# LayerNorm's running sums moved from VectorE to GpSimd, two channel tiles at a time, with the norm's chain and one pair's residuals placed differently at the seam

## The chip, the cores and the metric

The kernel runs on one core of a Trainium2 chip. The metric is the device time of one execution in microseconds; three timed runs of the kernel before gave 839.31, 839.94 and 841.18, so its time is the median, 839.94 us. Engines are named as in the profile: PE is TensorE (matmuls; PEld its weight loads), DVE VectorE, ACT ScalarE, POOL GpSimd, SP the queue that issues the loads.

## What is computed

Two residual layers on 256 tokens of width 2048, in float32. The first mixes eight retention heads and eight latent-attention heads; the second is a convolution module. The change lies where the first ends and in the second, whose reference is:

```python
def layer_conformer_conv(x, norm_g, w_in, conv_w, conv_b, ln_g, ln_b, w_out):
    h = rms_norm(x, norm_g)
    a, b, gate = jnp.split(h @ w_in, 3, axis=-1)
    u = a * jax.nn.sigmoid(b)
    u = lax.conv_general_dilated(u, conv_w[:, None, :], ..., feature_group_count=CONV_WIDTH) + conv_b
    u = jax.nn.silu(layer_norm(u, ln_g, ln_b))
    return x + (u * jax.nn.silu(gate)) @ w_out
```

The convolution is causal, has 31 taps and works on each of 2048 channels alone. `layer_norm` runs over the channels of a token: it needs, for each token, the sum of u and of u squared over all channels.

## The kernel before, in words

**Weights.** Float32 products are made of three matmuls of rounded parts (`mm3`, L193 to L195): high times high, high times low, low times high. A stream of weight units of 1 MB (128 x 2048) feeds them. For each half unit (128x1024) ScalarE writes the rounded copy `whi` (L167) and VectorE or GpSimd the residual `wlo` = raw - whi (L88, the helper of every tensor_tensor). Which of the two engines takes a unit's residuals is fixed when the unit is added to the stream (V or G). There are three raw buffers, five for `whi` and four for `wlo`; a residual is asked for three halves ahead of its use.

**Work order.** The order on TensorE, ScalarE and VectorE is written by the program itself. Each half unit is one tick of a clock in the program; `later(n, f)` puts f's instructions n ticks on, between the matmuls of that half. `pair(...)` makes 128x256 outputs of two 128-row tiles from two units: 96 matmuls, four halves, four ticks. GpSimd's and SP's order is not written out by hand.

**Seam 1.** The first layer ends with four `chunk`s. After each, VectorE adds the residual x1 (128x512, two token halves), ScalarE squares it with an accumulated sum (`x1_square`), TensorE transposes it (`x1_turn`, 8 matmuls), ScalarE writes its rounded copy `yh` (`y_hi`) and VectorE the rest `yl` (`y_lo`). After the last, `norm_x1` makes 1/rms: it loads ScalarE's table for Ln and Exp, VectorE reduces the sums, `rs_chain` takes Ln and Exp and one correction step (all 128x2), VectorE writes two 128x128 diagonals (L879), and `norm_rows` lets TensorE spread them over all rows (L884) and VectorE copies the result to R1. Each output of the second layer's input projection is multiplied by R1 (`norm_cols`). On TensorE the first pair of that projection is already running by then.

**Conv stage.** 16 pairs give a and b of channel tiles 0 to 15, eight more the gate. VectorE multiplies by R1, ScalarE takes the sigmoid (L1120), VectorE the product, then the 31 taps of the tile: one ScalarE instruction and some 30 of VectorE, each adding a shifted, weighted 128x256 tile to an accumulator in PSUM (L91). A planner (`pace`, `drain`, `spend`) puts so many taps into a tick as its costs allow; two tiles run interleaved. After tile 3, `shift` makes K, an estimate of the mean, and every tile has K subtracted when done (`centre`).

**Sums.** `centre_sq` lets ScalarE square a centred tile, and a tick later `centre_add` has VectorE add the tile and its square to running sums in PSUM (`run`, a bank of the four of the pool `mm`): two 128x256 adds per tile. Tile 15's adds write the result to SBUF (`sums`), the table for Ln and Exp is loaded, and LN_LAG = 4.5 ticks on `norm_conv` has TensorE sum over channels (L1030, L1031), VectorE and ScalarE make the mean and the factor (L1033 to `rs_chain`), and the steps `za` to `zc` (L1061 is one) make the split input of the last projection, two tiles at a time. Gate evaluations that fall between wait in `held`.

**Last projection.** Four banks over 16 tiles (`aux`), then two chunks, then the stores.

Of the kernel before, what the change touches and what calls it, by code (L numbers as in the profile page):

```python
# [10 lines left out]
AF = mybir.ActivationFunctionType  # L11
ALU = mybir.AluOpType
# [4 lines left out]
T = 256  # L17
# [10 lines left out]
TAP_US = 0.396  # L28
TICK_US = 2.88
X1_US = 5.0  # L30
LN_LAG = 4.5
WARM = 9
ENG = {mybir.EngineType.PE, mybir.EngineType.Activation, mybir.EngineType.DVE}
MAGIC = 12582912.0
# [14 lines left out]
def body(ctx, tc, a):  # L49
# [22 lines left out]
    def tmp(dt=F32):  # L72
        return tpool.tile([P, 512], dt, tag="t", name=nm("t"))
# [4 lines left out]
    def mmps():  # L78
        return psm.tile([P, 512], F32, tag="mm", name=nm("mm"))
# [7 lines left out]
    def tt(out, in0, in1, op, eng=None):  # L87
        (eng or V).tensor_tensor(out=out, in0=in0, in1=in1, op=op)  # L88
# [13 lines left out]
    def later(n, fn):  # L102
        due.append((clock[0] + n, len(due), fn))
# [117 lines left out]
            u_b[h] = st.add(a["w_qb"][h] if h < 3 else a["w_kvb"][(2, 3, 0, 1)[h - 3]], V)  # L221
    u_gate = [st.add(a["w_in"][20 + i], V) for i in range(16)]
    u_out = [st.add(a["w_out"][i], V) for i in range(16)]
    u_ab = [st.add(a["c_in"][i], V if i < 2 else G) for i in range(32)]
    u_cg = [st.add(a["c_in"][32 + i], G if i < 12 else V) for i in range(16)]
    u_co1 = [st.add(a["c_out1"][i], V) for i in range(8)]
    u_co2 = [st.add(a["c_out2"][i], V) for i in range(8)]

# [257 lines left out]
    def lnexp():  # L486
        nc.scalar.preload_act_table_set("natural_log_exp_and_others")
# [350 lines left out]
    ssq = small()  # L838

    def x1_square(c):  # L840
        for t in range(2):
            m = tmp()
            act(m[:, :], x1[t][:, c * 512:(c + 1) * 512], AF.Square, accum_out=ssq[:, 4 * t + c:4 * t + c + 1])
# [25 lines left out]
        later(1, lambda c=c: x1_turn(c))  # L869

    def norm_x1():
        lnexp()
        s = small()
        r = small()
        dg = tmp()
        V.tensor_reduce(out=s[:, 0:2], in_=ssq[:, 0:8].rearrange("p (t c) -> p t c", t=2), axis=AX.X, op=ALU.add)
        rs_chain(r[:, 0:2], s[:, 0:2], D)
        for t in range(2):
            V.tensor_scalar(out=dg[:, t * P:(t + 1) * P], in0=ident[:, :], scalar1=r[:, t:t + 1], scalar2=None, op0=ALU.mult)  # L879
        later(1.5, lambda: norm_rows(dg))  # L880
# [23 lines left out]
    def spend(us):  # L904
        budget[0] -= us
# [59 lines left out]
        drain()  # L965

    K = e1[:, 1024:1280]
    sums = e1[:, 512:1024]
    run = mmps()

    def ds(c):
        return kk(dd, c)
# [7 lines left out]
            centre_sq(c)  # L980

    def centre_sq(c):
        if c == 0:
            act(run[:, T:512], ds(c), AF.Square)
            V.tensor_copy(run[:, 0:T], ds(c))
        else:
            m = tmp()
            act(m[:, 0:T], ds(c), AF.Square)
            if c < 15:
                later(1, lambda: centre_add(c, m))  # L990
            else:
                centre_add(c, m)

    def centre_add(c, m):
        dst = sums if c == 15 else run
        tt(dst[:, 0:T], run[:, 0:T], ds(c), ALU.add)
        tt(dst[:, T:512], run[:, T:512], m[:, 0:T], ALU.add)
        spend(0.67)
        if c == 15:
            lnexp()  # L1000
            held.append([])
            later(LN_LAG, norm_conv)

    def shift():
        m = tmp()
# [21 lines left out]

    def norm_conv():
        lps = auxps()
        nc.tensor.matmul(lps[:, 0:T], ones[:, :], sums[:, 0:T], start=True, stop=True)  # L1030
        nc.tensor.matmul(lps[:, T:512], ones[:, :], sums[:, T:512], start=True, stop=True)  # L1031
        mu = tmp()
        V.tensor_scalar(out=mu[:, 0:T], in0=lps[:, 0:T], scalar1=1.0 / D, scalar2=None, op0=ALU.mult)  # L1033
        tt(mu[:, T:512], mu[:, 0:T], mu[:, 0:T], ALU.mult)
        stt(mu[:, T:512], mu[:, T:512], -float(D), lps[:, T:512], ALU.mult, ALU.add)
        ls = e1[:, 0:T]
# [12 lines left out]

        def zs(j):  # L1050
            for k in (2 * j, 2 * j + 1):
                act(ds(k), ds(k), AF.Silu, bias=cb[:, CB["lb"] + k:CB["lb"] + k + 1],
                    scale=cb[:, CB["lg"] + k:CB["lg"] + k + 1])

        def zb(j):
            o = (j % 4) * 512
            tt(pr(j), pr(j), cgt[j // 4][:, o:o + 512], ALU.mult)

        def zr(j):
            o = (j % 4) * 512  # L1060
            act(zh[j // 4][:, o:o + 512], pr(j), AF.Copy)  # L1061
# [229 lines left out]
```

## Time and profile before

| | us |
|---|---|
| median of three timed runs | 839.94 |
| the profiled execution | 841.35 |
| its span, first to last instruction | 839.6 |
| TensorE busy | 823.7 |
| VectorE busy | 628.7 |
| ScalarE busy | 422.1 |
| GpSimd busy | 207.4 |

All times of instructions are from the start of the span of the profiled execution. A line of the timeline gives start, duration, engine, line of the kernel, operation, output<-inputs, shape and count, and in brackets how long the engine had been idle and what ended that. In a list of waits stands: engine and what it was about to do <- what it waited for: total, times, longest. Busy time of TensorE overlaps within its pipeline, so waits and the start-to-start distance of matmuls say more than the busy share.

### The profile page before, as it was taken

The numbers are of one execution on the slowest core, as the hardware profiler recorded it, in microseconds if no ns is written. First come the engines' busy times: TensorE is split into PE (matmuls) and PEld (weight loads), VectorE is DVE, ScalarE is ACT, GpSimd is POOL, SyncE is SP. The second block draws the span as 40 slices with busy tenths as digits, with TensorE's granted clock in tenths as the row PEclk, the third lists the DMA queues.
The fourth block names the chain that finished last, engine by engine and source line by source line (L and its number), as shares of the span: only waits on it lengthen the run. The fifth ranks groups of instructions, "written<-read, shape, count | busy, mean of one in ns | idle before, by whom it ended". The sixth has DMA issues, their size and how long they took to land.

```text
span 839.6 us, 14612 instructions
## 1 busy us (share of the span) xinstructions
PE 823.7 (98%) x5856; PEld 779.3 (93%) x5856; DVE 628.7 (75%) x1147; ACT 422.1 (50%) x601; POOL 207.4 (25%) x115
## 2 busy tenths in 40 slices
PE   9999999999999999999999899999999999979998
PEld 8999999999999999988888899999999999967886
DVE  5887565798686755765554399999999999978752
ACT  6766444456456454654545344433544544456541
POOL 0000000000000000000002588885988885000000
PEclk9999999999999999999999899999999999989999
DMA  8965454444445334555554445544554554445650
GB/s 282 341 233 187 171 201 152 151 151 173 179 151 197 122 135 161 217 207 179 190 175 176 140 166 198 180 175 149 195 199 166 195 201 151 150 154 197 223 203 26
DMA packets 24116, 151.08 MB, mean 180 GB/s; under 512 B 2800, under 2 KB 3952, under 8 KB 6896
## 3 DMA queue, kind: packets, MB, share of 16 engines
q1 hardware_dynamic: 23616, 148.03, 49.6%
q0 software_dynamic: 288, 2.10, 0.6%
q8 instruction: 46, 0.75, 0.4%
q14 instruction: 22, 0.18, 0.1%
q10 hardware_dynamic: 144, 0.03, 0.0%
HBM read 148.04 MB, written 2.10 MB: 179 GB/s over the span
## 4 chain that ended last, share of the span: by engine, by line
PE 87%; DVE 9%; ACT 2%; DMA 1%; issue 1%; POOL 1%; SPq 0%; DVEq 0%; POOLq 0%; ACTq 0%
PE mm L195 26%; PE mm L193 25%; PE mm L194 25%; DVE aux L91 3%; PE aux L195 2%; PE aux L193 2%; PE aux L194 2%; DVE s L88 2%; DVE wlo L88 1%; DVE t L88 1%; DMA raw<-in_w_first 1%; DVE mm L88 1%; ACT whi L167 1%; POOL wlo L88 1%; PE aux L851 0%
## 5 line engine op out<-in xcount | busy, mean ns | idle before, releaser
L193 PE MATMUL mm<-s,whi 128*128 128x256 f32 x1404 | 402.6, 287 | 0.3 <-ACT whi L167 0.3
L195 PE MATMUL mm<-s,wlo 128*128 128x256 f32 x1404 | 398.9, 284 | 3.2 <-DVE wlo L88 2.1
L167 ACT ACTIVATE whi<-raw 128x1024 fp32r<-128x1024 f32 (+2 forms) x278 | 284.2, 1035 | 228.0 <-PE mm L194 94.2
L194 PE MATMUL mm<-s,whi 128*128 128x256 f32 x1404 | 398.2, 284 | 0.0
L88 DVE TENSOR_TENSOR wlo<-raw,whi 128x1024 fp32r<-128x1024 f32 (+2 forms) x194 | 227.9, 1183 | 99.0 <-PE mm L194 47.3
L195 PEld LDWEIGHTS mm<-s,wlo 128*128 128x128 f32 x1404 | 270.3, 192 | 4.4 <-DVE wlo L88 3.1
L193 PEld LDWEIGHTS mm<-s,whi 128*128 128x128 f32 x1404 | 270.5, 193 | 1.2 <-ACT whi L167 0.5
L194 PEld LDWEIGHTS mm<-s,whi 128*128 128x128 f32 x1404 | 270.4, 193 | 0.8
L88 POOL TENSOR_TENSOR wlo<-raw,whi 128x1024 fp32r<-128x1024 f32 x84 | 201.7, 2416 | 51.7 <-PE mm L195 25.4
L91 DVE SCALAR_TENSOR_TENSOR aux<-s,cb,aux 128x256 f32<-128x256 f32 x478 | 198.8, 484 | 11.8 <-ACT aux L916 9.1
L193 PE MATMUL mm<-whi,s 128*128 128x512 f32 (+1 forms) x376 | 134.3, 357 | 0.0
L194 PE MATMUL mm<-wlo,s 128*128 128x512 f32 (+1 forms) x376 | 133.6, 355 | 0.0
L195 PE MATMUL mm<-whi,s 128*128 128x512 f32 (+1 forms) x376 | 133.5, 355 | 0.0
L195 PEld LDWEIGHTS mm<-whi,s 128*128 128x128 f32 x376 | 70.6, 188 | 9.9
L194 PEld LDWEIGHTS mm<-wlo,s 128*128 128x128 f32 x376 | 70.7, 188 | 9.2
L193 PEld LDWEIGHTS mm<-whi,s 128*128 128x128 f32 x376 | 70.8, 188 | 9.0
L711 POOL MEMSET s<- 64x256 f32 x8 | 2.9, 361 | 232.1 <-PE mm L195 162.7
L1120 ACT ACTIVATE t<-mm 128x256 f32<-128x256 f32 x16 | 6.1, 384 | 53.9 <-DVE mm L88 53.9
L899 POOL MEMSET s<- 128x30 f32 x16 | 1.1, 121 | 116.8 <-PE mm L194 101.0
L193 PE MATMUL aux<-whi,s 128*128 128x512 f32 x64 | 26.0, 407 | 3.2 <-ACT s L1061 3.2
L195 PE MATMUL aux<-whi,s 128*128 128x512 f32 x64 | 26.6, 416 | 1.6 <-DVE s L88 1.6
L194 PE MATMUL aux<-wlo,s 128*128 128x512 f32 x64 | 25.8, 403 | 0.0
(190 smaller groups left out, 541.1 us busy)
## 6 DMA issues: line engine op xcount, KB each, us to landing
raw<-in_c_in SPq DMA_DIRECT2D x48, 1024.0 KB, 4.8
raw<-in_w_in SPq DMA_DIRECT2D x36, 1024.0 KB, 4.8
raw<-in_w_out SPq DMA_DIRECT2D x16, 1024.0 KB, 4.8
raw<-in_c_out SPq DMA_DIRECT2D x16, 1024.0 KB, 4.8
raw<-in_w_rv SPq DMA_DIRECT2D x8, 1088.0 KB, 5.1
raw<-in_w_kvb SPq DMA_DIRECT2D x4, 1024.0 KB, 4.8
raw<-in_w_first SPq DMA_DIRECT2D x7, 512.0 KB, 5.5
raw<-in_w_qb SPq DMA_DIRECT2D x3, 1024.0 KB, 4.7
```

The lines of the kernel that those rows point to most:

```text
L88: (eng or V).tensor_tensor(out=out, in0=in0, in1=in1, op=op)
L91: V.scalar_tensor_tensor(out=out, in0=in0, scalar=s, in1=in1, op0=op0, op1=op1)
L167: act(hi[:, :], self.raw[u][:, h * n:(h + 1) * n], AF.Copy)
L193: mm(ps, lh, rh, start=start, stop=False, skip_group_check=True)
L194: mm(ps, lh, rl, start=False, stop=False, skip_group_check=True)
L195: mm(ps, ll, rh, start=False, stop=stop, skip_group_check=True)
L711: G.memset(krz(i)[64 * b:64 * b + 64, :], 0.0)
L899: G.memset(upad(c, 0, TAPS - 1), 0.0)
L1120: act(sg[0][:, 0:T], ps[:, T:512], AF.Sigmoid)
```

## The change

Four edits:

1. The sums. They now lie in SBUF, in the tile `e1`: `sd` for u and `sv` for its square, each 128x512, two channel tiles side by side. GpSimd adds a pair of tiles at a time (`sums_pair`, pairs 1 to 6); pair 0 is ScalarE's own (a copy of 128x512 and two squares). VectorE folds the two halves (`sums_fold`) and adds tiles 14 and 15 itself. The bank `run` goes, and the planner is no longer charged 0.67 us per tile.
2. Residuals. The first four input units go to VectorE instead of the first two (the second pair's four residuals), and the first 14 of the gate's units to GpSimd instead of 12.
3. Seam 1. `norm_x1` runs one tick earlier, and its table load stands ahead of the last squares.
4. LN_LAG is 3.5 instead of 4.5.

```diff
-LN_LAG = 4.5
+LN_LAG = 3.5
...
-    u_ab = [st.add(a["c_in"][i], V if i < 2 else G) for i in range(32)]
-    u_cg = [st.add(a["c_in"][32 + i], G if i < 12 else V) for i in range(16)]
+    u_ab = [st.add(a["c_in"][i], V if i < 4 else G) for i in range(32)]
+    u_cg = [st.add(a["c_in"][32 + i], G if i < 14 else V) for i in range(16)]
...
     def x1_square(c):
+        if c == 3:
+            lnexp()
         for t in range(2):
...
     def norm_x1():
-        lnexp()
...
-    sums = e1[:, 512:1024]
-    run = mmps()
+    sd = e1[:, 0:512]
+    sv = e1[:, 512:1024]
...
-        if c == 0:
-            act(run[:, T:512], ds(c), AF.Square)
-            V.tensor_copy(run[:, 0:T], ds(c))
+        j, o = c // 2, (c % 2) * T
+        if c < 2:
+            act(sv[:, o:o + T], ds(c), AF.Square)
         else:
-            m = tmp()
-            act(m[:, 0:T], ds(c), AF.Square)
-            if c < 15:
-                later(1, lambda: centre_add(c, m))
-            else:
-                centre_add(c, m)
-
-    def centre_add(c, m):
-        dst = sums if c == 15 else run
-        tt(dst[:, 0:T], run[:, 0:T], ds(c), ALU.add)
-        tt(dst[:, T:512], run[:, T:512], m[:, 0:T], ALU.add)
-        spend(0.67)
+            if c % 2 == 0 or c == 15:
+                squares[c] = tmp()
+            act(squares[c if c > 13 else c - c % 2][:, (o if c < 14 else 0):(o if c < 14 else 0) + T], ds(c), AF.Square)
         if c == 15:
-            lnexp()
-            held.append([])
-            later(LN_LAG, norm_conv)
+            sums_end()
+        elif c == 14:
+            later(1, sums_14)
+        elif c % 2 == 1:
+            later(1, lambda: sums_pair(j))
+
+    def sums_pair(j):
+        d = dd[j // 4][:, (j % 4) * 512:(j % 4 + 1) * 512]
+        if j == 0:
+            act(sd, d, AF.Copy)
+        else:
+            tt(sd, sd, d, ALU.add, G)
+            tt(sv, sv, squares[2 * j][:, :], ALU.add, G)
+        if j == 6:
+            later(1, sums_fold)
+
+    def sums_fold():
+        if not folded:
+            tt(sd[:, 0:T], sd[:, 0:T], sd[:, T:512], ALU.add)
+            tt(sv[:, 0:T], sv[:, 0:T], sv[:, T:512], ALU.add)
+            folded.append(0)
...
-    later(2, norm_x1)
+    later(1, norm_x1)
```

**Seam 1 on ScalarE.** Before, from the copy of the third unit's first half (the names in the rows: `t_4744` and `t_4746` are the squares' outputs, `s_551` is `yh`, `m_4807` and `m_4809` hold the norm's two numbers; L487 loads the table for Ln and Exp, L886 that for the sigmoid):

```order
L167 ACTIVATE whi_4742<-raw_4647 128x1024
L843 ACTIVATE t_4744,m_4088<-s_537_3959 128x512
L843 ACTIVATE t_4746,m_4088<-s_538_3960 128x512
L167 ACTIVATE whi_4784<-raw_4647 128x1024
L857 ACTIVATE s_551_4083<-aux_4760,cb 128x256 x2
L857 ACTIVATE s_551_4083<-aux_4765,cb 128x256 x2
L487 ACT_TABLE_LOAD
L207 ACTIVATE m_4809<-m_4807 128x2
L208 ACTIVATE m_4809<-m_4809 128x2
L167 ACTIVATE whi_4838<-raw_4681 128x1024
L167 ACTIVATE whi_4866<-raw_4681 128x1024
L886 ACT_TABLE_LOAD
```

And in the changed kernel (lines there are numbered two higher in this part, and later ones more):

```order
L167 ACTIVATE whi_4741<-raw_4647 128x1024
L487 ACT_TABLE_LOAD
L845 ACTIVATE t_4744,m_4088<-s_537_3959 128x512
L845 ACTIVATE t_4746,m_4088<-s_538_3960 128x512
L207 ACTIVATE m_4776<-m_4774 128x2
L208 ACTIVATE m_4776<-m_4776 128x2
L167 ACTIVATE whi_4799<-raw_4647 128x1024
L859 ACTIVATE s_551_4083<-aux_4760,cb 128x256 x2
L859 ACTIVATE s_551_4083<-aux_4765,cb 128x256 x2
L167 ACTIVATE whi_4837<-raw_4681 128x1024
L887 ACT_TABLE_LOAD
L167 ACTIVATE whi_4869<-raw_4681 128x1024
```

The table load stands ahead of the squares, and Ln and Exp ahead of the next weight copy and the four `y_hi`.

**Seam 1 on VectorE.** Before, from the residual add of the last chunk's second half (`t_4805` are the diagonals, `s_553` is `yl`, `R_4087` is R1):

```order
L88 TENSOR_TENSOR s_538_3960<-mm_4554,s_538_3960 128x512
L88 TENSOR_TENSOR wlo_4738<-raw_4613,whi_4699 128x1024
L876 TENSOR_REDUCE m_4803<-m_4088 128x2
L85 TENSOR_SCALAR m_4807<-m_4803 128x2
L91 SCALAR_TENSOR_TENSOR m_4812<-m_4809 128x2
L88 TENSOR_TENSOR m_4812<-m_4812,m_4807 128x2
L91 SCALAR_TENSOR_TENSOR m_4804<-m_4812,m_4809 128x2
L879 TENSOR_SCALAR t_4805<-ident,m_4804 128x128 x2
L91 SCALAR_TENSOR_TENSOR s_553_4085<-aux_4760,cb,s_551_4083 128x256 x2
L91 SCALAR_TENSOR_TENSOR s_553_4085<-aux_4765,cb,s_551_4083 128x256 x2
L885 COPY R_4087<-aux_4868 128x256
L88 TENSOR_TENSOR mm_4737<-mm_4737,R_4087 128x512
```

And now, from the reduction on:

```order
L877 TENSOR_REDUCE m_4770<-m_4088 128x2
L85 TENSOR_SCALAR m_4774<-m_4770 128x2
L91 SCALAR_TENSOR_TENSOR m_4779<-m_4776 128x2
L88 TENSOR_TENSOR m_4779<-m_4779,m_4774 128x2
L91 SCALAR_TENSOR_TENSOR m_4771<-m_4779,m_4776 128x2
L880 TENSOR_SCALAR t_4772<-ident,m_4771 128x128 x2
L88 TENSOR_TENSOR wlo_4797<-raw_4647,whi_4741 128x1024
L91 SCALAR_TENSOR_TENSOR s_553_4085<-aux_4760,cb,s_551_4083 128x256 x2
L91 SCALAR_TENSOR_TENSOR s_553_4085<-aux_4765,cb,s_551_4083 128x256 x2
L88 TENSOR_TENSOR wlo_4833<-raw_4647,whi_4799 128x1024
L886 COPY R_4087<-aux_4839 128x256
L88 TENSOR_TENSOR wlo_4867<-raw_4681,whi_4837 128x1024
```

Four residuals (of the units `raw_4647` and `raw_4681`, which stood on GpSimd) stand between the diagonals and the first product; the fourth follows `mm_4736<-mm_4736,R_4087`.

**Seam 2 on VectorE.** Before, from the last product but two with R1 (`mm_7870`, the gate's sixth pair) to the norm (`aux_7228` is the accumulator of tile 15, `t_8061` its half with K, `s_659` the centred tile, `e_4086` the sums):

```order
L88 TENSOR_TENSOR mm_7870<-mm_7870,R_4087 128x512
L88 TENSOR_TENSOR wlo_8021<-raw_7797,whi_7985 128x1024
L91 SCALAR_TENSOR_TENSOR aux_7228<-s_657_4717,cb,aux_7228 128x256 x4
L88 TENSOR_TENSOR wlo_8056<-raw_7873,whi_8025 128x1024
L91 SCALAR_TENSOR_TENSOR aux_7228<-s_657_4717,cb,aux_7228 128x256 x3
L88 TENSOR_TENSOR t_8061<-t_8061,e_4086 128x256
L88 TENSOR_TENSOR s_659_4735<-aux_7228,t_8061 128x256
L88 TENSOR_TENSOR e_4086<-mm_4736,s_659_4735 128x256
L88 TENSOR_TENSOR e_4086<-mm_4736,t_8067 128x256
L88 TENSOR_TENSOR wlo_8096<-raw_7873,whi_8058 128x1024
L88 TENSOR_TENSOR wlo_8126<-raw_7945,whi_8100 128x1024
L88 TENSOR_TENSOR mm_8020<-mm_8020,R_4087 128x512
```

And now, from the product of the gate's fifth pair (`mm_7721`) on:

```order
L88 TENSOR_TENSOR mm_7721<-mm_7721,R_4087 128x512
L91 SCALAR_TENSOR_TENSOR aux_7229<-s_657_4717,cb,aux_7229 128x256 x5
L88 TENSOR_TENSOR e_4086<-e_4086,s_659_4735 128x256
L88 TENSOR_TENSOR e_4086<-e_4086,t_7846 128x256
L91 SCALAR_TENSOR_TENSOR aux_7229<-s_657_4717,cb,aux_7229 128x256 x7
L88 TENSOR_TENSOR t_7922<-t_7922,e_4086 128x256
L88 TENSOR_TENSOR s_659_4735<-aux_7229,t_7922 128x256
L88 TENSOR_TENSOR e_4086<-e_4086,s_659_4735 128x256
L88 TENSOR_TENSOR e_4086<-e_4086,t_7958 128x256
L88 TENSOR_TENSOR mm_7874<-mm_7874,R_4087 128x512
L88 TENSOR_TENSOR wlo_8047<-raw_7877,whi_8021 128x1024
L1060 TENSOR_SCALAR t_8066<-aux_8063 128x256
```

The sums end ahead of the product of the gate's sixth pair (`mm_7874`) instead of behind it, and the residuals `wlo` that stood among the last taps are gone. On TensorE the norm's two matmuls stand 36 matmuls into the gate's seventh pair; before, they stood 36 into the eighth.

**GpSimd.** Its first adds in the changed kernel (`e_4086<-e_4086,s_...` adds two centred tiles, `...,t_...` two squares):

```order
L88 TENSOR_TENSOR wlo_6187<-raw_5993,whi_6146 128x1024
L88 TENSOR_TENSOR e_4086<-e_4086,t_6157 128x512
L88 TENSOR_TENSOR wlo_6226<-raw_5993,whi_6189 128x1024
L88 TENSOR_TENSOR e_4086<-e_4086,s_658_4734 128x512
L88 TENSOR_TENSOR wlo_6263<-raw_6067,whi_6230 128x1024
L88 TENSOR_TENSOR e_4086<-e_4086,s_658_4734 128x512
L88 TENSOR_TENSOR wlo_6301<-raw_6067,whi_6265 128x1024
L88 TENSOR_TENSOR e_4086<-e_4086,t_6160 128x512
```

Before, the twelve adds were not there; the residuals follow each other alike.

More of the change, by code (lines that the diff above doesn't have):

```diff
@@ L967, in body @@
     K = e1[:, 1024:1280]
-    sums = e1[:, 512:1024]
-    run = mmps()
+    sd = e1[:, 0:512]
+    sv = e1[:, 512:1024]
+    squares = {}
+    folded = []
     def ds(c):
@@ L982, in centre_sq, with sums_14, sums_end @@
     def centre_sq(c):
-        if c == 0:
-            act(run[:, T:512], ds(c), AF.Square)
-            V.tensor_copy(run[:, 0:T], ds(c))
-        else:
-            m = tmp()
-            act(m[:, 0:T], ds(c), AF.Square)
-            if c < 15:
-                later(1, lambda: centre_add(c, m))
-            else:
-                centre_add(c, m)
-    def centre_add(c, m):
-        dst = sums if c == 15 else run
-        tt(dst[:, 0:T], run[:, 0:T], ds(c), ALU.add)
-        tt(dst[:, T:512], run[:, T:512], m[:, 0:T], ALU.add)
-        spend(0.67)
-        if c == 15:
-            lnexp()
-            held.append([])
-            later(LN_LAG, norm_conv)
+        j, o = c // 2, (c % 2) * T
+        if c < 2:
+            act(sv[:, o:o + T], ds(c), AF.Square)
+        else:
+            if c % 2 == 0 or c == 15:
+                squares[c] = tmp()
+            act(squares[c if c > 13 else c - c % 2][:, (o if c < 14 else 0):(o if c < 14 else 0) + T], ds(c), AF.Square)
+        if c == 15:
+            sums_end()
[17 more added lines that the diff above has]
+            folded.append(0)
+    def sums_14():
+        sums_fold()
+        if len(folded) < 2:
+            tt(sd[:, 0:T], sd[:, 0:T], ds(14), ALU.add)
+            tt(sv[:, 0:T], sv[:, 0:T], squares[14][:, 0:T], ALU.add)
+            folded.append(0)
+    def sums_end():
+        sums_14()
+        tt(sd[:, 0:T], sd[:, 0:T], ds(15), ALU.add)
+        tt(sv[:, 0:T], sv[:, 0:T], squares[15][:, 0:T], ALU.add)
+        lnexp()
+        held.append([])
+        later(LN_LAG, norm_conv)
     def shift():
@@ L1029, in norm_conv @@
         lps = auxps()
-        nc.tensor.matmul(lps[:, 0:T], ones[:, :], sums[:, 0:T], start=True, stop=True)
-        nc.tensor.matmul(lps[:, T:512], ones[:, :], sums[:, T:512], start=True, stop=True)
+        nc.tensor.matmul(lps[:, 0:T], ones[:, :], sd[:, 0:T], start=True, stop=True)
+        nc.tensor.matmul(lps[:, T:512], ones[:, :], sv[:, 0:T], start=True, stop=True)
         mu = tmp()
@@ L1035, in norm_conv @@
         stt(mu[:, T:512], mu[:, T:512], -float(D), lps[:, T:512], ALU.mult, ALU.add)
-        ls = e1[:, 0:T]
+        ls = e1[:, T:512]
         rs_chain(ls, mu[:, T:512], D)
```

## The prediction

> **What bounds the kernel now.** I read the page first, then the waits of TensorE, then the clock by stage, then the timeline around each long wait.
>
> ```profile
> PE   9999999999999999999999899999999999979998
> PEclk9999999999999999999999899999999999989999
> ```
>
> TensorE is full in all slices but two places, and its clock falls in the same two. So the time is that of TensorE's stream, plus its waits, plus what a reduced clock adds. The list of waits, longest first, names all that are long:
>
> ```profile
> PE aux L193 <- ACT s L1061: 3.2, 1, 3.2
> PE aux L884 <- DVE t L879: 2.9, 1, 2.9
> PE mm L195 <- DVE wlo L88: 2.1, 4, 1.3
> PE aux L195 <- DVE s L88: 1.6, 1, 1.6
> PE mm L195 <- POOL wlo L88: 1.1, 1, 1.1
> ```
>
> The clock by windows (columns: length, then busy time of PE, PEld, DVE, ACT, POOL, then granted clock, DMA share, GB/s):
>
> ```profile
> 457.13:463.96 6.83, 4.62 (x39) 4.41 (x37) 3.59 (x4) 6.27 (x10) 5.89 (x3) 1.00 0.37 122
> 463.96:470.79 6.83, 6.14 (x27) 5.99 (x28) 2.45 (x7) 0.07 (x1) 0.27 (x1) 0.50 0.24 98
> 737.09:743.92 6.83, 3.66 (x27) 3.08 (x26) 5.87 (x9) 6.77 (x10) 0.00 (x0) 1.00 0.35 120
> 743.92:750.75 6.83, 5.24 (x13) 4.11 (x13) 4.83 (x7) 2.42 (x5) 0.00 (x0) 0.50 0.64 239
> ```
>
> Behind the 2.9 us wait and behind the 3.2 us wait, TensorE is granted half its clock for 6.83 us. Work done at half clock takes twice as long, so 6.14/2 = 3.07 us and 5.24/2 = 2.62 us are lost on top of the waits. The waits of 1.3 and 1.1 us bring no such window. Thus seam 1 (layer 0 to layer 1) costs 2.9 + 3.07 = 5.97 us, and seam 2 (LayerNorm to the last projection) 1.33 + 3.17 + 1.59 + 2.62 = 8.71 us; one wait of 1.05 us on GpSimd lies between.
>
> The Trainium skill (TensorE: Matmul & The Clock Gate, "What's actually happening") puts the fall to half clock after at least one idle window of about 3.4 us. The trace disagrees: here a wait of 2.9 us came before one. By the page's rule neither wait would have cost its half clock, and the sum below would be 10.0 instead of 15.7 (rival 5).
>
> **Seam 1.** Rows of the four engines around it:
>
> ```profile
> 452.30 1.06 ACT L167 ACTIVATE whi<-raw 128x1024 fp32r<-128x1024 f32 x1 [1.66 <-PE mm L195]
> 453.88 0.61 ACT L843 ACTIVATE t<-s 128x512 f32<-128x512 f32 x1
> 454.32 0.36 PE L193 MATMUL mm<-s,whi 128*128 128x256 f32 x1
> 454.81 0.17 DVE L85 TENSOR_SCALAR m<-m 128x2 f32<-128x2 f32 x1
> 458.50 1.28 ACT L487 ACT_TABLE_LOAD   x1
> 460.03 0.20 ACT L208 ACTIVATE m<-m 128x2 f32<-128x2 f32 x1
> 459.01 2.41 POOL L88 TENSOR_TENSOR wlo<-raw,whi 128x1024 fp32r<-128x1024 f32 x1 [0.47 <-ACT s L857]
> 460.27 1.17 DVE L91 SCALAR_TENSOR_TENSOR m<-m 128x2 f32<-128x2 f32 x1 [5.29 <-ACT m L208]
> 461.86 2.65 DVE L879 TENSOR_SCALAR t<-ident,m 128x128 f32<-128x128 f32 x2
> 461.88 2.34 POOL L88 TENSOR_TENSOR wlo<-raw,whi 128x1024 fp32r<-128x1024 f32 x1 [0.47 <-DVE m L91]
> L879 DVE TENSOR_SCALAR t<-ident,m x2: 273/1362/2452, 461.9 to 464.2; 128x128 f32<-128x128 f32 x2
> 461.35 0.28 PE L194 MATMUL mm<-s,whi 128*128 128x256 f32 x1
> 461.47 0.28 PE L195 MATMUL mm<-s,wlo 128*128 128x256 f32 x1
> 464.65 1.19 PE L884 MATMUL aux<-t,ones 128*128 128x256 f32 x2 [2.90 <-DVE t L879]
> ```
>
> Two things are late. The table load stands behind a weight copy and four evacuations, so Ln and Exp end at 460.23 though their input was ready at 454.98. Then VectorE's two-element instruction takes 1.17 us and the first diagonal 2.45 us where the second takes 0.27: each ends when GpSimd's residual ends (461.42, 464.22).
>
> The change puts the load ahead of the squares, the norm one tick (one half of a weight unit) earlier, and that pair's four residuals on VectorE, behind the diagonal. New sum: copy ends 453.36, load 1.28 to 454.64, two squares and their reads some 1.3 (as 453.26 to 454.58 before) to 455.96, reduce and scale 0.4 to 456.4, Ln and Exp 0.45 to 456.85, three small operations of 0.16 with gaps to 457.45, diagonal 2 x 0.27 to 458.0. TensorE's order now has the broadcast (L884) 36 matmuls behind the transposes instead of 60; they start 0.12 us apart, so it comes up at 454.32 + 36 x 0.12 = 458.64. Spare: about 0.6 us. I take a wait of 0 (0 to 1). The four moved residuals cost VectorE 4 x 1.2 us where it was idle; the first is due at the next pair's start near 465 and done near 459.3; the evacuations behind it on ScalarE, and then on VectorE, end near 461, and TensorE needs them at 454.32 + 60 x 0.12 + 0.5 = 462. Seam 1 gains 5.97.
>
> The Trainium skill (ScalarE: Activation LUTs, "What ACT_TABLE_LOAD costs") adds a drain of about 1.38 us to each load. The trace shows none: this load ends at 459.78 and Ln starts at 459.80. By the page the diagonal would come 0.8 us late and the gain be 5.2.
>
> **The sums.** What VectorE pays now, and what the residuals cost on each engine:
>
> ```profile
> L88 DVE TENSOR_TENSOR mm<-mm,t 128x256 f32<-128x256 f32 x14 | 6.1, 433 | 1.5
> L88 DVE TENSOR_TENSOR mm<-mm,s 128x256 f32<-128x256 f32 x14 | 6.0, 429 | 0.1
> L88 DVE TENSOR_TENSOR wlo<-raw,whi 128x1024 fp32r<-128x1024 f32 x9 | 10.9, 1218 | 0.8 <-ACT whi L167 0.8
> L88 POOL TENSOR_TENSOR wlo<-raw,whi 128x1024 fp32r<-128x1024 f32 x81 | 194.6, 2417 | 46.8 <-PE mm L195 21.6 <-ACT whi L167 17.6 <-issue 6.9
> 471.00:728.00 257.00, 255.95 (x2132) 255.69 (x2131) 243.10 (x571) 112.70 (x147) 194.59 (x81) 1.00 0.50 177
> ```
>
> In the conv stage VectorE is busy 243 of 257 us: it runs nearly level with TensorE. The change takes the 28 adds in PSUM (12.1 us) and the last two (0.85) from it and gives it six of 128x256 back (fold, tile 14, tile 15: 6 x 0.42 = 2.5). It also moves the last gate units' residuals to GpSimd: five of 1.22 us (6.1) stood ahead of the end of the sums. VectorE is some 16.5 us lighter there.
>
> GpSimd gets twelve adds of 128x512. No row shows one; VectorE does that shape in 0.69, GpSimd twice the shape in 2.42, so 0.7 to 2.4; I take half of GpSimd's own row, 1.2. Four residuals take 9.7 of a pair's 96 x 0.12 = 11.52 us, so two pairs leave 3.7 us for two adds of 1.2. A residual may be written three halves (8.6 us) before its use, so it is ready up to 6.2 us early. That cushion hides the adds. ScalarE's extra copy of 128x512 (0.6 us) is hidden by its idle half.
>
> **The middle.**
>
> ```profile
> 569.99 5.37 DVE L88 TENSOR_TENSOR s<-s,e 128x256 f32<-128x256 f32 x4
> 586.10 0.69 DVE L88 TENSOR_TENSOR mm<-mm,R 128x512 f32<-128x512 f32 x1
> 587.10 1.05 ACT L167 ACTIVATE whi<-raw 128x1024 fp32r<-128x1024 f32 x1
> 588.29 4.76 POOL L88 TENSOR_TENSOR wlo<-raw,whi 128x1024 fp32r<-128x1024 f32 x2 [6.29 <-ACT whi L167]
> ```
>
> GpSimd waited 6.3 us for a copy that stood on ScalarE behind a sigmoid, and that waited for VectorE, which had eight sum adds in a row and a copy first. Without them (9 x 0.43 with gaps, 4.4 us) the residual ends near 586.9, three adds of GpSimd's included, and TensorE needs it at 589.5: the 1.05 us go.
>
> **Seam 2.**
>
> ```profile
> 728.96 0.42 DVE L88 TENSOR_TENSOR e<-mm,t 128x256 f32<-128x256 f32 x1
> 731.86 0.60 PE L1030 MATMUL aux<-e,ones 128*128 128x256 f32 x2
> 735.34 0.42 DVE L1033 TENSOR_SCALAR t<-aux 128x256 f32<-128x256 f32 x1
> 738.85 0.42 DVE L91 SCALAR_TENSOR_TENSOR e<-t,t 128x256 f32<-128x256 f32 x1
> 742.58 0.61 ACT L1061 ACTIVATE s<-s 128x512 fp32r<-128x512 f32 x1
> 743.25 0.50 PE L193 MATMUL aux<-whi,s 128*128 128x512 f32 x1 [3.17 <-ACT s L1061]
> ```
>
> The chain from the sums (729.38) over the norm's factor (739.27) to the first split tile (743.19) ends 3 us after TensorE wants it. In the new order TensorE's norm matmuls stand one whole pair earlier, 11.5 us. VectorE must have the sums 11.5 + 1.3 (the wait that goes) - 2.5 (729.38 to 731.86) = 10.3 us sooner, and is 16.5 lighter: 6.2 to spare. Against that stands GpSimd, which now works beside the last adds: each group of VectorE operations with both inputs in SBUF can be held as in the row at 569.99 (four of 0.42 took 5.37 us, 3.7 too many in two waits). Four such groups at 1 us each leave 2 us. I take no wait. Then 11 us of cover lie between the chain and its use, the z steps keep that lead, and the pair's residuals come from GpSimd, six us early: all four parts go, 8.71.
>
> **Sum.** 5.97 + 1.05 + 8.71 = 15.7 us; I leave 0.2 for small waits: 15.5. The profiled execution took 841.35 (span 839.6 and 1.75 around it), 1.4 above the median of 839.94; against the median: 839.94 - 15.5 = 824.4.
>
> **Rivals.**
> 1. *The sums come late.* If the four groups are held as long as the worst row shows (2.2 each, 8.8 in all), TensorE waits 2.6 us at the norm matmuls and may lose another 3.1 to half clock: 827.0 to 830.1. For it: GpSimd is busy until pair 22's residuals. Against: the operations within a group follow each other freely once it is let in. 0.16.
> 2. *Seam 1 is not freed.* If the 1.17 and 2.45 us were not GpSimd's doing, the diagonal comes at 458.0 + 3.2, 2.6 us late, and the half clock stays: 824.4 + 5.7 = 830.1. Against: both end with GpSimd's instruction to 0.1 us. 0.06.
> 3. *Slower: GpSimd becomes the bound.* It falls behind by 2(X - 1.86) per two pairs over six pairs of pairs, less the cushion of 6.2. To eat 15.5 us an add must cost X = 1.86 + (15.5 + 6.2)/12 = 3.67 us; above that the kernel is slower, at 4.2 us 846. Even the double-sized row is at 2.42. 0.02.
> 4. *Nothing gained*: the waits reappear elsewhere, 839.9. 0.02.
> 5. *The half clock outlives the waits*, because something else at the seams brings it: 839.94 - (15.5 - 5.7) = 830.1. Against: it follows the two longest waits and no other place. 0.02. The page on the clock gate in the Trainium skill, named above, would have it so.
>
> **Numbers.** The forecast has 0.72. Its own range is 823.0 (each restart after a wait also lost some 0.1 to 0.3) to 826; with rival 1's main part up to 829.0. About 0.2% (1.7 us) can be told from no change. Faster 0.96, same 0.02, slower 0.02.
>
> **What would show it.** After: no long wait at the norm broadcast and no half clock near 459 to 471; first diagonal near 0.27 us; GpSimd's adds near 1.2 us; no wait near 584 for a residual; the wait for L1061 gone, norm factor ready some 15 us before the last projection starts. Wrong if GpSimd's adds near 3.7 us, or if TensorE waits for VectorE's sums by more than 2 us.

## The result and the profile after

The changed kernel takes 826.75 us (median of 4 runs, 826.25 to 827.08); the kernel before, on the same chip, 839.62 us (4 runs, 838.11 to 841.18). The ratio is 0.9846 [0.9827, 0.9865]: 12.9 us less, where 15.5 less was forecast. It lies 0.75 us above the forecast's own range of 823.0 to 826, and inside the range that includes the first rival (to 829.0). The profiled execution of the changed kernel took 826.25 us, with a span of 824.5 and 1.75 around it.

The page's slices of TensorE and of its granted clock, after:

```profile
PE   8999999999999999999999999999999999999998
PEclk9999999999999999999999999999999999999999
```

Both dents of before are gone from both rows. TensorE's waits, longest first (total, times, longest):

```profile
PE aux L1057 <- DVE e L88: 1.8, 1, 1.8
PE aux L243 <- POOL ones L236: 1.0, 1, 1.0
PE mm L193 <- ACT whi L167: 1.0, 2, 0.5
PE mm L195 <- DVE wlo L88: 0.8, 3, 0.3
```

The waits for the split tile (3.2), for the diagonals (2.9), for the first product's sum (1.6) and for GpSimd's residual (1.1) are all gone. One is new: the norm's matmuls, which add up the sums over the partitions, wait 1.8 us for VectorE's last sum. The second row is at the kernel's start and was there before.

Seam 1 after, rows of the timeline (start, duration):

```profile
453.69 1.28 ACT L487 ACT_TABLE_LOAD   x1
456.99 0.20 ACT L208 ACTIVATE m<-m 128x2 f32<-128x2 f32 x1
457.22 0.16 DVE L91 SCALAR_TENSOR_TENSOR m<-m 128x2 f32<-128x2 f32 x1 [0.51 <-ACT m L208]
457.81 0.48 DVE L880 TENSOR_SCALAR t<-ident,m 128x128 f32<-128x128 f32 x2
458.90 0.28 PE L195 MATMUL mm<-s,wlo 128*128 128x256 f32 x1
459.02 0.60 PE L885 MATMUL aux<-t,ones 128*128 128x256 f32 x2
```

The two-element operation takes 0.16 us where it took 1.17, the two diagonals 0.48 together where they took 2.65. They are done at 458.29, and the broadcast (L885) starts at 459.02, 0.12 behind the matmul ahead of it: no wait. The clock stays at 1.00.

GpSimd's adds, grouped by tile (lowest, median and highest ns, first and last start):

```profile
L88 POOL TENSOR_TENSOR e<-e,t x6: 1291/1300/1318, 570.3 to 691.4; 128x512 f32<-128x512 f32 x6
L88 POOL TENSOR_TENSOR e<-e,s x6: 1281/1294/1307, 574.0 to 690.1; 128x512 f32<-128x512 f32 x6
```

Seam 2 after, VectorE's six SBUF sums (tile `e`), what GpSimd ran beside them, and TensorE's new wait; then the first matmul of the last projection and the first of the stage behind it:

```profile
693.14 4.74 DVE L88 TENSOR_TENSOR e<-e 128x256 f32<-128x256 f32 x2
703.57 0.83 DVE L88 TENSOR_TENSOR e<-e,s 128x256 f32<-128x256 f32 x1
704.32 2.62 DVE L88 TENSOR_TENSOR e<-e,t 128x256 f32<-128x256 f32 x1
711.73 2.01 DVE L88 TENSOR_TENSOR e<-e,s 128x256 f32<-128x256 f32 x1
713.66 0.41 DVE L88 TENSOR_TENSOR e<-e,t 128x256 f32<-128x256 f32 x1
692.66 7.49 POOL L88 TENSOR_TENSOR wlo<-raw,whi 128x1024 fp32r<-128x1024 f32 x3
701.71 4.95 POOL L88 TENSOR_TENSOR wlo<-raw,whi 128x1024 fp32r<-128x1024 f32 x2 [1.55 <-ACT whi L167]
710.93 2.52 POOL L88 TENSOR_TENSOR wlo<-raw,whi 128x1024 fp32r<-128x1024 f32 x1 [4.28 <-ACT whi L167]
713.79 0.70 PE L1057 MATMUL aux<-e,ones 128*128 128x256 f32 x2 [1.77 <-DVE e L88]
733.47 0.40 PE L193 MATMUL aux<-whi,s 128*128 128x512 f32 x1
777.01 0.39 PE L193 MATMUL mm<-whi,s 128*128 128x512 f32 x1
```

An undisturbed add of this shape takes 0.41 us (713.66). The fold's two took 4.74, tile 14's 0.83 and 2.62, and tile 15's first 2.01. That first one ends at 713.74, 0.29 behind GpSimd's residual, which ends at 713.45; in the same way tile 14's second ends at 706.94, 0.28 behind a residual that ends at 706.66. The fold's two stand beside three residuals in a row. Together 10.61 us stand where six free adds take 2.5: 8.1 us of hold. The last projection (its first matmul to the first of the next stage) lasts 777.01 - 733.47 = 43.54 us. Before, its start is the prediction's row at 743.25, and its end is this row of the timeline of the kernel before:

```profile
792.14 0.39 PE L193 MATMUL mm<-whi,s 128*128 128x512 f32 x1
```

That is 48.89 us, so 5.35 us came off behind the wait for the split tile.

### The profile page after: what moved, and what is told of

Its sections match the earlier page's. It is cut to its first block, busy times and chain, and to the rows that moved or that the text cites. A ratio compares the mean times of both kernels' runs of the same rounds, so it can differ in the third digit from the quotient of the medians.

```text
span 824.5 us, 14589 instructions
## 1 busy us (share of the span) xinstructions
PE 816.1 (99%) x5856; PEld 774.5 (94%) x5856; DVE 624.3 (76%) x1122; ACT 423.7 (51%) x602; POOL 222.9 (27%) x127
## 4 chain that ended last, share of the span: by engine, by line
PE 74%; DVE 23%; issue 1%; DMA 1%; ACT 1%; POOL 0%; SPq 0%; DVEq 0%; POOLq 0%; ACTq 0%
PE mm L195 21%; PE mm L194 21%; PE mm L193 21%; DVE aux L91 16%; DVE s L88 2%; PE aux L194 2%; PE aux L195 2%; PE aux L193 2%; DVE e L88 1%; DVE mm L88 1%; DVE t L88 1%; DMA raw<-in_w_first 1%; DVE wlo L88 1%; PE aux L853 0%; PE aux L661 0%
## 5 line engine op out<-in xcount | busy, mean ns | idle before, releaser
L193 PE MATMUL aux<-whi,s 128*128 128x512 f32 x64 | 24.9, 389 | 0.0
```

Source lines behind the costliest of these rows:

```text
L193: mm(ps, lh, rh, start=start, stop=False, skip_group_check=True)
```

## The experiments

Theory: the gain is the sum of three independent parts (seam 1 by the placing and the residuals, the middle and seam 2 by the sums), each by taking a wait and the half clock behind it away. Rival A: the residuals alone, or the placing alone, free seam 1. Rival B: the new wait at the norm matmuls comes from GpSimd's adds being slow, or from what the edit put ahead of them, and not from too short a lead. Every ratio is against the kernel before on the same chip, whose median lies between 839.62 and 840.21 us in all these comparisons, so times of different experiments can be set side by side to about half a microsecond.

**The kernel before once more.** No edit.

> The kernel before once more, for a second profile and more times. My theory (each long wait of TensorE brings one window of 6.83 us at half clock): the waits of 2.9 us at the norm broadcast and 3.2 us at the last projection are there again, and a half-clock window behind each or nearly each; where a window falls differently on the wait, up to 3 us of the time come and go. Rival (the windows belong to the two places, not to the waits): they stand at the same places with the same length whatever the waits do. Time 838 to 841.5.

Measured: 840.16 us (838.47 to 842.1), ratio 1.0 [0.9987, 1.0013]. Its profile (838.83 us) has the same waits as the one shown ahead of the prediction:

```profile
PE aux L193 <- ACT s L1061: 3.2, 1, 3.2
PE aux L884 <- DVE t L879: 2.9, 1, 2.9
```

But the clock by windows at seam 1 reads otherwise (length, busy PE, PEld, DVE, ACT, POOL, granted clock, DMA share, GB/s):

```profile
460.62:467.45 6.83, 3.92 (x31) 3.70 (x30) 6.03 (x10) 3.74 (x6) 4.01 (x2) 1.00 0.44 154
467.45:474.28 6.83, 6.83 (x59) 6.83 (x58) 1.13 (x2) 2.39 (x3) 4.51 (x2) 1.00 0.25 66
```

The wait of 2.9 us lies in the first window, and the second has the full clock: no half clock. Seam 2's wait had its half clock in this execution too. So a wait of the same length is followed by half clock in one execution and not in another; the rival, a window that stands at the place whatever the waits do, falls for seam 1. Half clock that comes and goes can make 3 of the 5 us by which the runs of the kernel before scatter: of its 59 executions in these experiments, the 15 with a mean granted clock of 0.995 took 838.7 us on average, the nine with 0.992 or less 841.7.

**The residuals alone.**

```
-    u_ab = [st.add(a["c_in"][i], V if i < 2 else G) for i in range(32)]
+    u_ab = [st.add(a["c_in"][i], V if i < 4 else G) for i in range(32)]
```

> The kernel before with one edit: the second pair's four residuals on VectorE instead of GpSimd. My theory (GpSimd's residuals held the norm's chain): first small operation 0.16 instead of 1.17 us, first diagonal 0.27 instead of 2.45, diagonals done near 461.4 just when TensorE comes (461.6), so the 2.9 us wait falls to under 0.5 and the half clock goes: 5.5 to 6 us faster. Rival (the table load's place is what counts): Ln and Exp still end at 460.2, the wait stays over 2 us, less than 1 us faster.

Measured: 835.95 us (835.17 to 837.07), ratio 0.9954 [0.9938, 0.9971], 4.2 us less, where I had expected 5.5 to 6. The wait at the norm broadcast is gone. VectorE at seam 1:

```profile
460.70 0.16 DVE L91 SCALAR_TENSOR_TENSOR m<-m 128x2 f32<-128x2 f32 x1 [2.69 <-ACT m L208]
461.28 0.48 DVE L879 TENSOR_SCALAR t<-ident,m 128x128 f32<-128x128 f32 x2
```

With no residual on GpSimd, both operations take their free time, with nothing else changed: the hold was GpSimd's doing. The chain is still as late as before (460.70 against 460.27), but without the holds it comes in time. The residuals alone free seam 1.

**The placing alone** (the norm one tick earlier, the table load ahead of the last squares).

```
     def x1_square(c):
+        if c == 3:
+            lnexp()
...
     def norm_x1():
-        lnexp()
...
-    later(2, norm_x1)
+    later(1, norm_x1)
```

> The kernel before with one edit: the norm one tick earlier and its table load ahead of the last squares; the four residuals stay on GpSimd. My theory: the first small operation is held to GpSimd's end at 458.5 and a diagonal to 461.4, so the diagonals come near 461.7 while TensorE now wants them at 458.6: a wait near 3 us and half clock behind it, 0 to 1 us from the kernel before. Rival (placing suffices): no wait, 5.5 to 6 us faster.

Measured: 837.74 us (836.89 to 839.48), ratio 0.9977 [0.9966, 0.9988], 2.4 us less. I had expected a wait near 3 and 0 to 1 us of difference; the wait is 1.4:

```profile
PE aux L885 <- DVE t L880: 1.4, 1, 1.4
```

```profile
456.59 2.32 DVE L85 TENSOR_SCALAR m<-m 128x2 f32<-128x2 f32 x1
460.00 0.48 DVE L880 TENSOR_SCALAR t<-ident,m 128x128 f32<-128x128 f32 x2
456.49 2.40 POOL L88 TENSOR_TENSOR wlo<-raw,whi 128x1024 fp32r<-128x1024 f32 x1 [3.87 <-ACT t L845]
460.40 2.40 POOL L88 TENSOR_TENSOR wlo<-raw,whi 128x1024 fp32r<-128x1024 f32 x1 [1.52 <-ACT whi L167]
```

One operation of two elements is still held, from 456.59 to 458.91, to the end of GpSimd's residual at 458.89. But the next residual starts only at 460.40, since its weight copy now stands behind Ln and Exp on ScalarE, and the diagonals pass in the gap. I had left that out. A wait of 1.4 brought no half clock in this execution.

**Both, without the sums.** The two edits above together.

> The kernel before with both edits of seam 1 (residuals and placing), sums as before. My theory: no wait over 0.3 us at the norm broadcast, no half clock there, 5.9 us faster; seam 2 as before with its waits of 1.3, 3.2 and 1.6 us and its half clock. Rival (a window of half clock belongs to the place): the window near 464 stays and only 2.9 us are gained.

Measured: 835.93 us (834.46 to 836.37), ratio 0.9951 [0.9933, 0.9968]: 4.2 us less, where the sum had 5.97. No wait at the broadcast; seam 2 is as it was:

```profile
PE aux L193 <- ACT s L1062: 3.2, 1, 3.2
```

The placing adds nothing that can be told on top of the residuals (835.93 against 835.95).

**The sums alone.** The changed kernel with seam 1's three edits undone, gate units 12 and 13 on VectorE again, and the norm's lag at 4.5 ticks as before; the norm matmuls then stand 60 matmuls into the gate's seventh pair.

```
-LN_LAG = 3.5
+LN_LAG = 4.5
...
-    u_ab = [st.add(a["c_in"][i], V if i < 4 else G) for i in range(32)]
-    u_cg = [st.add(a["c_in"][32 + i], G if i < 14 else V) for i in range(16)]
+    u_ab = [st.add(a["c_in"][i], V if i < 2 else G) for i in range(32)]
+    u_cg = [st.add(a["c_in"][32 + i], G if i < 12 else V) for i in range(16)]
...
-    later(1, norm_x1)
+    later(2, norm_x1)
```

> The kernel before with one edit: the sums by GpSimd, two tiles at a time (fold and tiles 14 and 15 on VectorE); residuals, the norm's place at seam 1 and the lag of 4.5 ticks as before. My theory (VectorE's sum adds delayed the middle and seam 2): the 1.05 us wait in the middle goes, the norm's two matmuls stand most of a pair earlier, the 3.2 and 1.6 us waits at the last projection and their half clock go, a wait of 0 to 3 us comes at the norm's matmuls; seam 1 as before. 6 to 9.5 us faster than the kernel before. Rival (moved sums gain only together with the gate's residuals on GpSimd): under 3 us faster.

Measured: 828.36 us (827.37 to 828.93), ratio 0.9857 [0.9839, 0.9876], 11.8 us less; I had expected 6 to 9.5. Its one long wait is seam 1's, in the profiled execution (827.37 us) again without half clock; two of its four executions, at 828.9 us, have a mean granted clock of 0.998 where the profiled one has 1.000:

```profile
PE aux L884 <- DVE t L879: 2.9, 1, 2.9
```

So the sums alone gain 11.8 where seam 1 alone gains 4.2, and more than the 9.76 (middle and seam 2) of the prediction's sum.

**The new wait: the lead of the norm matmuls.** The changed kernel with one number changed, one tick more and half a tick less.

```
-LN_LAG = 3.5
+LN_LAG = 4.5
```

```
-LN_LAG = 3.5
+LN_LAG = 3.0
```

> The changed kernel with the lag of 4.5 ticks as before: the norm's matmuls stand 24 matmuls (2.9 us) later. My theory (the 1.77 us wait there is for held adds, and behind the norm there is spare time): the wait goes and nothing replaces it, 1.5 to 2 us faster than the changed kernel, near 824.9. Rival (the chain behind the norm has no spare time): a wait of 1 to 3 us at the last projection, 826.7 or slower.

> The changed kernel with a lag of 3.0 ticks: the norm's matmuls stand 12 matmuls (1.44 us) earlier. The wait there becomes 1.77 + 1.44 = 3.2 us. My theory (half clock follows a long wait, wherever it lies, if enough of it falls into one 3.4 us stretch): a half-clock window of 6.83 us appears there, 3 us more in all or nearly all runs: 826.75 + 1.44 + 3 = 831.2. Rival (half clock belongs to the seams' other work): no window, 828.2.

Measured: 824.92 us (824.17 to 825.69), ratio 0.9818 [0.98, 0.9836], with 4.5; 830.61 us (829.98 to 833.74), ratio 0.9891 [0.9874, 0.9909], with 3.0. With 4.5 no wait at the norm matmuls is left, and the time falls by 1.8, the length of the wait. With 3.0 the wait is 3.2 and a half clock follows it:

```profile
PE aux L1057 <- DVE e L88: 3.2, 1, 3.2
```

```profile
709.53:716.36 6.83, 4.38 (x37) 4.18 (x35) 6.13 (x11) 2.61 (x4) 2.55 (x2) 1.00 0.44 154
716.36:723.18 6.82, 6.07 (x24) 5.70 (x25) 5.66 (x8) 3.50 (x5) 2.78 (x2) 0.50 0.25 73
```

The sum for it is 1.4 more wait and 6.07/2 = 3.0 of half clock, 4.4 on top of 826.75: 831.2. The median came to 830.6. The profiled execution is the slowest of the six, 833.74 us, and has a second, shorter window of half clock near the kernel's start (33.69 to 37.10); the five others, 829.98 to 831.09, have a mean granted clock of 0.995 to 0.997 where the changed kernel has 1.000, so they lost clock too, but how much of it at this wait is not shown.

**The new wait: the gate's residuals.** The changed kernel with gate units 12 and 13 on VectorE, as before the change.

```
-    u_cg = [st.add(a["c_in"][32 + i], G if i < 14 else V) for i in range(16)]
+    u_cg = [st.add(a["c_in"][32 + i], G if i < 12 else V) for i in range(16)]
```

> The changed kernel with the gate's units 12 and 13 back on VectorE. GpSimd then ends near 702. My theory (GpSimd's residuals hold VectorE's adds with both inputs in SBUF: 4.74 for two of 0.42, then 2.62 and 2.01): the two groups behind 702 shrink to 0.42 each, which gives back some 4 of the 4.9 us that the four residuals cost VectorE; the wait at the norm's matmuls is 2 to 3 us, 0 to 1.5 us slower than the changed kernel, more where half clock follows. Rival (the long adds are not GpSimd's doing): they stay long, the wait is near 6.7 us with half clock, 836.

Measured: 824.37 us (824.27 to 824.7), ratio 0.9812 [0.9795, 0.9829]. I had expected up to 1.5 slower, since the residuals load VectorE; it is 2.4 faster than the changed kernel. VectorE's sums and residuals there:

```profile
693.51 4.74 DVE L88 TENSOR_TENSOR e<-e 128x256 f32<-128x256 f32 x2
703.94 0.42 DVE L88 TENSOR_TENSOR e<-e,s 128x256 f32<-128x256 f32 x1
704.27 0.42 DVE L88 TENSOR_TENSOR e<-e,t 128x256 f32<-128x256 f32 x1
704.61 1.22 DVE L88 TENSOR_TENSOR wlo<-raw,whi 128x1024 fp32r<-128x1024 f32 x1
709.70 1.22 DVE L88 TENSOR_TENSOR wlo<-raw,whi 128x1024 fp32r<-128x1024 f32 x1
711.74 0.42 DVE L88 TENSOR_TENSOR e<-e,s 128x256 f32<-128x256 f32 x1
712.19 0.42 DVE L88 TENSOR_TENSOR e<-e,t 128x256 f32<-128x256 f32 x1
```

GpSimd is done by then, so tile 14's and tile 15's adds take their free time, and only the fold is held. VectorE pays two residuals (2.4 us) ahead of the sums' end and is spared 4.2 us of hold. No wait at the norm matmuls is left. At a lag of 3.5 ticks it is these residuals on GpSimd that bring the wait; the prediction had booked moving the gate's last residuals as 6.1 us of relief for VectorE.

**Both undone.** Lag 4.5 and gate units 12 and 13 on VectorE.

```
-LN_LAG = 3.5
+LN_LAG = 4.5
...
-    u_cg = [st.add(a["c_in"][32 + i], G if i < 14 else V) for i in range(16)]
+    u_cg = [st.add(a["c_in"][32 + i], G if i < 12 else V) for i in range(16)]
```

> The changed kernel with two edits undone: the gate's units 12 and 13 back on VectorE and the lag of 4.5 ticks. My theory: with either alone no wait over 0.5 us is left on TensorE, so both together bring nothing more, 824.2 to 825.0, the same as with the residuals alone. Rival (there is still a hidden gain in the lag): below 823.8.

Measured: 824.74 us (824.17 to 825.95), ratio 0.9825 [0.9808, 0.9842]: nothing on top of either one, so both remove the same wait. The version with the gate units alone undone, 824.37 us, is the fastest of all here, but the three without the wait lie within 0.6 us of each other, which is not told apart.

**GpSimd's price.** The changed kernel with two more adds of 128x512 behind each of GpSimd's twelve; what they add up is read by nobody.

```
             tt(sd, sd, d, ALU.add, G)
+            for _ in range(2):
+                tt(spare[:, 0:512], d, d, ALU.add, G)
             tt(sv, sv, squares[2 * j][:, :], ALU.add, G)
+            for _ in range(2):
+                tt(spare[:, 0:512], d, d, ALU.add, G)
```

> The changed kernel with each of GpSimd's twelve adds followed by two more of the same size whose result nobody reads, so that an add costs 3 x 1.30 = 3.9 us. The prediction's sum for a GpSimd that falls behind (spare 1.86 us per add, cushion 6.2 us): 12 x (3.9 - 1.86) - 6.2 = 18.3 us more, 845; TensorE then waits for GpSimd's residuals, first at pairs 10 and 11 where four adds lie close together. Rival (GpSimd's queue has more room than the sum says, since waits of one pair are made up in the next): under 8 us more. At 1.30 us each, as in the changed kernel, both say that the adds cost nothing.

Measured: 839.07 us (838.2 to 840.39), ratio 0.9988 [0.9977, 0.9998], 12.3 us more than the changed kernel, where I expected 18.3. The extra adds, which read one tile as both inputs, took less than I had reckoned with, and TensorE now waits for GpSimd's residuals:

```profile
L88 POOL TENSOR_TENSOR s<-s x24: 1029/1040/1103, 570.1 to 709.0; 128x512 f32<-128x512 f32 x24
```

```profile
PE mm L195 <- POOL wlo L88: 8.8, 5, 4.8
PE aux L1062 <- DVE e L88: 1.4, 1, 1.4
```

```profile
588.14:594.97 6.83, 5.53 (x26) 5.53 (x27) 6.79 (x19) 2.38 (x4) 6.83 (x4) 0.50 0.43 155
```

With 1.30 + 2 x 1.04 = 3.38 us per add, the formula of the prediction's third rival gives 12 x (3.38 - 1.86) - 6.2 = 12.0 us, against 12.3 measured. So that rival's mechanism exists. That its price came out to 0.3 us is partly luck: the waits for GpSimd sum to 8.8, not 12.0, and another 5.53/2 = 2.8 is half clock (behind the longest wait, in the last row), which the formula does not have. The changed kernel, with an add at 1.30, stays clear of falling behind by 0.56 us per add.

## Why the prediction held, and where it did not

**In all.** Seam 1 alone gained 4.2 us and the sums alone 11.8; together 16.0, and the version without the new wait gained 15.8. So the parts add up, and the forecast of 15.5 was nearly that of a kernel without a new wait. That it was so near is luck: two terms were off by about 2 us, in opposite directions, and a wait was left out. The changed kernel is 2.4 us above that version: 1.8 of it is the wait (1.9 by the last column of the table below), and some 0.5 is not placed.

TensorE runs 5856 matmuls in every version, so the starts of the same matmul in two traces show where time goes (starts in the timeline, subtracted; one profiled execution each):

| us from matmul to matmul | 3200th to 3400th (seam 1) | 3400th to 4400th (middle) | 4400th to 5800th (seam 2, last projection) |
|---|---|---|---|
| kernel before, half clock at seam 1 | 30.07 | 121.49 | 213.55 |
| kernel before again, none there | 27.32 | 121.49 | 212.91 |
| sums alone | 27.32 | 120.18 | 203.33 |
| changed kernel | 24.18 | 120.18 | 205.31 |
| gate units 12 and 13 on VectorE | 24.18 | 120.18 | 203.41 |

**Seam 1: the mechanism right, the term too large.** 5.97 was booked, 4.2 measured; the same difference appears from the sums-only kernel to the one with the gate units undone (828.36 - 824.37 = 4.0). The mis-sized part is the 3.07 us of half clock. It was read from one execution, which had both half clocks and took 1.4 us more than the median, and was then taken in full from the median. For that execution the term holds: by the table 30.07 - 24.18 = 5.89 us went. Without half clock 27.32 - 24.18 = 3.14 went. Of the three profiles with this wait of 2.9 us (the kernel before twice, the sums alone once) only the one that the prediction read shows the half clock. If the median gain is 2.9 plus a share of 3.07, then 4.2 makes the share about 0.4; that is an estimate, since the executions that were not profiled have no clock by stages on record. Every other step of seam 1 held: the load's place, 0.16 and 0.48 us for the held operations (0.16 and 0.54 assumed), the broadcast 0.73 us behind its diagonals (0.6 of spare forecast). That both of the things it called late had to be mended was not so: the residuals alone gained as much as both edits together.

**The middle: right.** No wait for GpSimd's residual is left there; by the table 1.3 us went, where 1.05 was booked.

**The sums on GpSimd: right in kind, price 8% low.** 1.2 was estimated, 1.30 measured, and the cushion hid all twelve.

**Seam 2: "I take no wait" failed.** The prediction counted 6.2 us to spare and took off four groups of held operations at 1 us each. The groups were held 8.1 us in all, near the 8.8 of its first rival; the wait was 1.8 where that rival had 2.6, and the second part of that rival, the half clock, did not come. The prediction's argument against that rival, that operations within a group follow each other freely, did not hold: the fold's two took 4.74 beside three residuals. The step that failed is the price of the hold, 4 us taken and 8.1 measured: 6.2 - 8.1 is 1.9 too little, and the wait is 1.8. Behind it stands the relief of 6.1 us by moving the last gate units' residuals: it counted what VectorE no longer runs, but not that each moved residual then holds VectorE's SBUF adds. The run with those units put back shows it: both late groups at 0.42 + 0.42 us, and no wait. There two residuals (2.4 us) stand ahead of the sums' end, so moving them spared VectorE 2.4 us and cost it 4.2 of hold. The longer lag removes the wait as well, so it was the shorter lead and the hold together. Against it stands that the old losses of seam 2 and the middle were undercounted: 9.76 booked, 11.8 measured. Of the 2.0 between them 1.1 lies in the last projection's stage (5.35 gained by the two traces, where 1.59 and 2.62 were booked), and by the table 0.3 each in the middle and in the rest of seam 2 (213.55 - 203.41 = 10.1 gained there without the new wait, where 8.71 were booked). The last 0.3 has no place; before the change acts, at the 400th matmul, these executions already differ by up to 0.9 us.

**Lead of the norm.** The factor was forecast some 15 us ahead of the last projection. It is ready at 721.99, 11.5 us ahead of 733.47, which is the 11 us of cover that the prediction wrote elsewhere. The new wait takes nothing from this lead, since it delays the last projection alike. From the norm's matmuls (713.79) it is 19.7 us to the last projection and 8.2 to the factor, 1.4 of it because GpSimd's last residual held VectorE's own to 2.58 us where a free one takes 1.22; without that the lead would be near 13, an estimate from these rows, so 15 was too high:

```profile
715.55 2.58 DVE L88 TENSOR_TENSOR wlo<-raw,whi 128x1024 fp32r<-128x1024 f32 x1 [0.87 <-issue]
721.57 0.42 DVE L91 SCALAR_TENSOR_TENSOR e<-t,t 128x256 f32<-128x256 f32 x1
720.63 1.28 ACT L1065 ACT_TABLE_LOAD   x1
721.92 0.60 ACT L1173 ACTIVATE s<-mm 128x512 f32<-128x512 f32 x1
```

The last two rows bear on the drain of about 1.38 us that the Trainium skill (ScalarE: Activation LUTs, "What ACT_TABLE_LOAD costs") adds to a load: this one ends at 721.91 and the next operation starts at 721.92. The trace does not agree, as in the kernel before, and at seam 1 the lower gain of 5.2 worked out from that figure has nothing to stand on: that gain came out lower for another reason.

**The rivals.** The first happened in its main part, inside the range. The second, the fourth and the fifth fell: the kernel with the residuals moved and nothing else changed shows the held operations free, and with the waits the half clocks went. In the kernel before run again the same wait at seam 1 had no half clock, which also speaks against the fifth. The third did not happen, by the measured price.

## What to carry to other kernels

When work moves from one engine to another, ask not only who is relieved but whom the receiver then holds up: here each residual on GpSimd could hold VectorE's SBUF-to-SBUF adds for most of its 2.4 us, so the last stretch before a chain that TensorE waits for is best kept free of GpSimd. A loss that follows a wait by chance, as half clock does, should be booked at its share over several executions, not at what one profile shows. Parts measured alone and then added show which estimate was off even where the total fits.

## What the runs showed of the hardware

**When half clock follows a wait.** Leaving out the last microseconds of the kernel, the profiles here show nine windows with half clock, eight of 6.83 us and one of 3.41, and their starts fit a grid of 3.41 us per execution. All but one go by how much of one 3.41 us stretch TensorE idles, and not by the length of the wait:

| wait of TensorE, us | idle ahead of the grid's edge, us | half clock |
|---|---|---|
| 713.91 to 717.10 (lag 3.0) | 2.45 to 716.36 | yes |
| 740.08 to 743.25 (kernel before) | 2.81 to 743.86 | yes |
| 738.15 to 741.32 (kernel before again) | 2.36 to 740.51 | yes |
| 461.74 to 464.65 (kernel before) | 2.2 to 463.96 | yes |
| 734.65 on (residuals alone) | 2.02 to 736.67 | yes |
| 1.77 (changed kernel) | 1.77, whole in one stretch | no |
| 462.62 to 465.53 (kernel before again) | 1.41, then 1.5 | no |
| 462.03 to 464.93 (sums alone) | 1.74, then 1.16 | no |
| 1.4 (placing alone) | 1.4 at most | no |
| 0.84 and 0.76 (lag 3.0, near the kernel's start) | 1.60 to 33.69 | yes, 3.41 us |

The row of the changed kernel (its window by the grid; TensorE busy 1.65 of 3.42):

```profile
711.60:715.02 3.42, 1.65 (x11) 1.34 (x10) 3.04 (x4) 3.26 (x4) 2.23 (x2) 1.00 0.00 0
```

By all rows but the last the limit lies between 1.77 and 2.02 us of idle in 3.41. The last row does not fit:

```profile
30.28:33.69 3.41, 1.81 (x13) 1.40 (x12) 2.16 (x3) 3.25 (x5) 0.00 (x0) 1.00 0.72 303
33.69:37.10 3.41, 3.41 (x18) 3.41 (x18) 3.41 (x4) 3.41 (x5) 0.00 (x0) 0.50 0.51 135
```

There two short waits left 1.60 us idle and half clock followed. The ends of matmuls are modelled in the profile, so its idle time is itself uncertain; what else counts stays open. A wait of 2.9 that straddles an edge can stay under the limit on both sides, which fits its half clock coming in some executions only. Where an execution shows no half clock at a place, the edge there is reckoned on from those that are recorded, so the rows with "no" rest on that inference. The Trainium skill (TensorE: Matmul & The Clock Gate, "What's actually happening") asks for a whole idle window of about 3.4 us; these runs show less than two thirds of one to be enough.

**GpSimd's two-input operations.** An add of 128x512 fp32 takes 1.30 us, and 1.04 where both inputs are the same tile; a residual of 128x1024 takes 2.4.

**Holds.** A VectorE operation of 0.16 us took up to 2.32 while a GpSimd instruction ran, and 0.42 up to 2.62; the first ends 0.02 us behind GpSimd's instruction, the second 0.28. Held were operations with all inputs in SBUF: those of two elements, the diagonals, the adds and VectorE's own residuals.
